# Attention of the prompt's first three heads moved from the gather loop into the input projections, in a one-core transformer step

## The chip, the cores and the metric

The kernel runs on one core of a Trainium2 chip. A core has five engines with instruction queues of their own, each of which takes its instructions in the order written: TensorE (PE; its weight loads are shown as PEld), VectorE (DVE), ScalarE (ACT), GpSimd (POOL) and SyncE (SP, here a queue of DMA issues). The metric is the device time of one execution in microseconds (us); lower is better. The kernel before takes 2638.99 us, the median of three runs (2634.69 to 2639.50).

## The reference

One inference step of a trunk with two layers, for a prompt of 256 tokens and 8 sample sequences of 4 new tokens with a paged cache of 2048 tokens. Layer 0 mixes tokens by sparse attention, layer 1 by a convolution module; each is followed by a convolutional feed-forward network. The change is in layer 0 alone. For the prompt it computes, per block of 128 queries:

```python
p = x @ w_in                              # q (16 heads), k and v (4 heads), qi (16 x 64), ki (64), wi (16)
q, k, qi, ki = rope_all(q, k, qi, ki, pos)
dots  = jnp.einsum('thd,sd->ths', qi, ki)
score = jnp.einsum('th,ths->ts', wi * IDX_W_SCALE, relu(dots))
_, idx = top_k(where(causal, score, -inf), 64)            # each query keeps 64 keys
s = einsum('tngd,tsnd->tngs', q, k[idx]) * HEAD_DIM ** -0.5
o = einsum('tngs,tsnd->tngd', softmax(where(valid, s, -inf)), v[idx])
y = o.reshape(T, 2048) @ w_out
```

For the sample tokens it is the same with 256 selected keys out of 2052 each, which are read from the paged cache by index. Prompt and samples go through all weight matrices together, as 288 columns (256 + 32).

## The kernel before

**Weights.** All weights are fp32 and are multiplied in three passes: a slab of weights (128 x 1024) is loaded (`raw`), split into a high part on ScalarE (`wh`, L166) and a low part on VectorE or, for slabs with the flag `pool`, on GpSimd (`wl`, L168), and multiplied at L245 to L247 (`wh` by the high half of x, `wh` by the low half, `wl` by the high half). `pump` (L142) issues loads up to five slabs ahead and splits up to three ahead.

**Lanes.** The order of instructions is written out by hand (a manual schedule). `gemm` (L258) emits a projection's matmuls and calls `tick` (L184) after every few of them with their planned time. `tick` gives that time as credit to each of a list of lanes. A lane is a queue of generators; each `yield` names the time after which the next piece of work may be emitted between the projection's matmuls. `drain` (L197) emits all that is left in a lane at once.

**Layer 0, projections.** The order is index keys, k (`g_k`), index queries (two groups), q (four groups of 512 columns, one group per key head), v (two groups of 256 columns). A q group has 8 slabs, a v group 4. A group's results are copied out of PSUM by ScalarE (`evac_rope`, L729: staging copies L733, full copies L735), rotated on VectorE (L738 to L743) and copied back by ScalarE (L747). Beside them run as lanes: the prompt's index (`prompt_index`, its top 64 by eight rounds of max and replace, with the mask `pm` at L1083 and L1084), and `sample_index`, which finds for each sample token its 256 best keys: a bisection in 31 steps (L923 on VectorE, a count over partitions on TensorE at L902, L933, L934), then a compaction into a list of row numbers (L941 to L1022), whose last step writes `idxS` (L1029) and calls `kv_load`. After the second v group `drain` finishes these lanes.

**Gathers.** `kv_load` (L771) issues per sample token two gathers of 128 rows of 4 KB (512 KB each) on GpSimd (L672), with a small memset (`pause`, L786) behind each. The buffers are a ring of 11: four of `kvA`, three of `kvB`, and four that lie over xh and xl, the halves of x, once the projections are done. A buffer comes free when the value matmuls of its token are done.

**Layer 0, loop.** For each of 32 sample tokens t (L1351): `keys(t)` transposes the gathered keys on TensorE (L1251, two groups of four) and copies them out (L1254 VectorE, L1256 ScalarE); `scores(t - 1)` multiplies them (L1272); after each four tokens comes a softmax, and `values` (L1315, and L1320 to L1327) emits the products with the gathered values in steps between later tokens. Between these steps `fill(FILL)` emits pieces of `filler` (L1184): the prompt's attention, as eight units of one key head (four query heads) and one tile of 128 tokens. A unit adds the mask and the scores in PSUM (L1200, L1201), takes the row maximum on VectorE (L1202, L1204), the exponential with its row sum on ScalarE (L1206), the reciprocal and the scaling of the weights on VectorE (L1210, L1212), transposes the weights on TensorE (L1227, copied out by ScalarE at L1229), multiplies with the values (L1223) and copies the result out (L1232). In the filler the scores of one unit are emitted ahead of the transposes and the value product of the unit before it. At token 24 `pump` is called for the out-projection; by then two of its slabs have been split during the second v group. After the loop the attention's output is split (L1374, L1375) and the out-projection begins.

Of the kernel before, what the change touches and what calls it, by code (L numbers as in the profile page):

```python
# [39 lines left out]
FILL = 0.45  # L40
# [10 lines left out]
HEAD = 2.0  # L51
# [3 lines left out]
LST = (2.5, 2.5, 2.5, 1.6, 1.2, 0.9)  # L55
# [61 lines left out]
class K:  # L117
    def __init__(self, ctx, tc, a, o):
# [8 lines left out]
        self.slabs = []  # L127
        self.n_dma = self.n_split = self.pos = 0
# [12 lines left out]

    def pump(self, i):  # L142
        nc = self.nc
        while True:
            if self.n_dma < min(len(self.slabs), i + self.R) and self.n_dma < self.n_split + self.R:
                s = self.slabs[self.n_dma]
                r = self.wraw.tile([128, 1024], F32, name="raw")
                v = r[:, :s.kt * s.C].rearrange("p (k c) -> p k c", c=s.C)
                off = 0
                for w, c0, n in s.segs:  # L150
                    src = w[s.k0 * 128:(s.k0 + s.kt) * 128, c0:c0 + n].rearrange("(k p) c -> p k c", p=128)
                    nc.sync.dma_start(v[:, :, off:off + n], src)
                    off += n
                self.raw[self.n_dma] = r
                self.n_dma += 1
            elif self.n_split < min(self.n_dma, i + self.S):
                s = self.slabs[self.n_split]
                n = s.kt * s.C
                r = self.raw.pop(self.n_split)
                if s.plain:  # L160
                    self.sp[self.n_split] = (r, None)
                    self.n_split += 1
                    continue
                wh = self.wsp.tile([128, 1024], F32R, name="wh")
                wl = self.wsp.tile([128, 1024], F32R, name="wl")
                nc.scalar.activation(wh[:, :n], r[:, :n], AF.Copy)  # L166
                eng = nc.gpsimd if s.pool else nc.vector
                eng.tensor_tensor(wl[:, :n], r[:, :n], wh[:, :n].bitcast(F32), op=OP.subtract)  # L168
                if not s.pool:
                    self.v(1.1)  # L170
                self.sp[self.n_split] = (wh, wl)
                self.n_split += 1
            else:
                break
# [376 lines left out]
def trunk(ctx, tc, a, o, stages=9):  # L551
# [72 lines left out]
    stB = ExitStack()  # L624
# [26 lines left out]
    con = bp.tile([128, NCO], F32, name="con")  # L651
# [54 lines left out]
    R = bp.tile([128, 4, T], F32, name="rsh")  # L706
# [61 lines left out]
    kvt = {"pos": 0, "done": 0, "cap": 4}  # L768
    RING = 4 + NKVB + 4

    def kv_load(done):  # L771
        kvt["done"] += done
        while kvt["pos"] < min(kvt["done"] + kvt["cap"], NS * TS):
            t = kvt["pos"]
            i = t % RING
            if i < 4:
                g = kvA.tile([128, 2, 1024], F32, name="kvt")
            elif i in (7, 8, 9):
                g = kvt["B"].tile([128, 2, 1024], F32, name="kvt")
            else:  # L780
                g = kvt["B2"][i // 6][:, i // 5 % 2 if i < 6 else i // 10]
# [67 lines left out]
    def sample_index():  # L849
# [179 lines left out]
        nc.vector.tensor_scalar(idxS, p[:, :64], 0.25, None, op0=OP.add)  # L1029
        kv_load(0)  # L1030
# [4 lines left out]
    def prompt_index(half):  # L1035
# [35 lines left out]
        for tt in range(2):  # L1071
# [14 lines left out]
            yield PRI  # L1086

# [30 lines left out]
    q = base.tile([128, NT, T], F32, name="x")  # L1118

    def post_q(h):  # L1120
        return lambda: nc.scalar.activation(qn[:, h], q[:, 4 * h:4 * h + 4, TP:].rearrange("p g t -> p t g"), AF.Copy)

    for gi in range(4):
# [3 lines left out]
    vT = bp.tile([128, 8, T], F32, name="qi")  # L1127

    def turn_v(gi):

        for tt in range(3):
            n = 128 if tt < 2 else 32
            p = pb()
            for m in range(2):
                nc.tensor.transpose(p[:n, m * 128:m * 128 + 128], vT[:, 2 * gi + m, tt * 128:tt * 128 + n], ident)
            dst = vt[:, tt] if tt < 2 else vs
            nc.scalar.activation(dst[:, 256 * gi:256 * gi + 256], p[:n, :256], AF.Copy)
            yield 0.6

    for gi in range(2):  # L1140
# [8 lines left out]
    nc.sync.dma_start(o["v"][:TP].rearrange("(a p) c -> p a c", p=128), vt)  # L1149
    nc.sync.dma_start(o["v"][TP:], vs)  # L1150
    k.lanes.remove(kxl)
    k.lanes.remove(pl_)
    k.fine = False
    stB.close()
# [4 lines left out]
    stC = ExitStack()  # L1159
    cp = stC.enter_context(tc.tile_pool(name="att", bufs=2))  # L1160
    kvB = stC.enter_context(tc.tile_pool(name="kvB", bufs=NKVB))
# [6 lines left out]
    ot = q  # L1168
# [11 lines left out]
    kvt["B"] = kvB  # L1180
    kvt["B2"], kvt["cap"] = [base.tile([128, 2, 2, 1024], F32, name="kvx", tag=n) for n in ("xh", "xl")], RING
    kv_load(0)

    def filler():  # L1184
        units = [(tt, h) for tt in range(2) for h in range(4)]
        st_ = {}

        def qk(u):
            tt, h = u
            nk = 128 * (tt + 1)  # L1190
            per = 512 // nk
            P = cp.tile([128, 4, nk], F32, name="P")
            mx = cp.tile([128, 4], F32, name="mx")
            sm = cp.tile([128, 4], F32, name="sm")
            for b0 in range(0, 4, per):
# [40 lines left out]
        for n in range(len(units) + 1):  # L1236
            if n < len(units):
                yield from qk(units[n])
            if n:
                yield from pv(units[n - 1])  # L1240
# [688 lines left out]
```

## Time and profile before

| | |
|---|---|
| median of three runs | 2638.99 us |
| the profiled execution | 2612.4 us, of which the span from first to last instruction is 2610.6 us |
| instructions | 49517 |
| mean granted clock of TensorE | 0.993 of full speed |
| TensorE busy, share of the span | 97% |
| VectorE, ScalarE, GpSimd | 62%, 45%, 25% |
| projections of layer 0 | from the start to 272 us |
| loop of layer 0 up to the first out-projection matmul | 272 to 398 us |

The profile is of one execution. Its page gives busy times per engine, a chain of waits followed back from the last instruction, and groups of instructions by line. Rows of the stage view give, for a stretch from A to B, its length, then for PE, PEld, DVE, ACT and POOL the busy time with the number of instructions in brackets, then the granted clock, the busy share of the DMA engines and their rate in GB/s. Rows of a timeline give start, duration, engine, line, operation, and in square brackets how long the engine had been idle and what it had waited for. Rows of groups give line, engine, operation, shapes and count, then total busy time and the mean of one in ns, then idle time ahead of them. Rows of the wait view give who waited for whom: total, number, longest. TensorE's instructions overlap, so that the duration of one is longer than the distance to the next.

### The profile page before, as it was taken

Reading aid. Unit: us, or ns where it says so; the run is one execution under the profiler, and the core shown is the slowest. Engines: PE = TensorE matmul, PEld = TensorE weight load, DVE = VectorE, ACT = ScalarE, POOL = GpSimd, SP = SyncE. Lnnn points to the kernel's source line nnn. Section 1 sums busy time; section 2 is a strip of 40 time slices with the busy share of each in tenths; the row PEclk is TensorE's granted clock in tenths of the full one; section 3 lists DMA queues with packets and bytes.
Section 4 is the critical chain, followed back from the end, with each engine's and each line's share of the span. In section 5 each row is a group of like instructions: output and inputs, shape, how many; then the busy total and the mean of one; then the engine's idle time right before and its main releaser. Section 6 shows DMA issues by size and latency. Waiting matters only on the chain.

```text
span 2610.6 us, 49517 instructions
## 1 busy us (share of the span) xinstructions
PE 2540.9 (97%) x19572; PEld 2445.5 (94%) x19572; DVE 1611.6 (62%) x2525; ACT 1163.7 (45%) x1811; POOL 643.3 (25%) x917
## 2 busy tenths in 40 slices
PE   8999899999999999999998998999999999999997
PEld 8889669999999999999998897999999999999997
DVE  4577446686665445555659887768555444655554
ACT  4444444464443334443446444656444333444334
POOL 2042661442221101011236543343110000111123
PEclk9999999999999999999999999999999999999999
DMA  9935875555555555556555675565555555555653
GB/s 341 205 109 153 298 273 169 164 182 180 166 169 162 154 176 162 168 162 163 172 161 144 166 191 145 178 173 163 170 160 171 160 157 171 163 168 167 162 167 104
DMA packets 410329, 454.91 MB, mean 174 GB/s; under 512 B 34816, under 2 KB 338096, under 8 KB 408944
## 3 DMA queue, kind: packets, MB, share of 16 engines
q1 hardware_dynamic: 397696, 400.66, 51.9%
q0 software_dynamic: 12400, 51.09, 5.8%
q8 instruction: 153, 2.51, 0.4%
q14 instruction: 80, 0.66, 0.1%
HBM read 438.37 MB, written 13.30 MB: 173 GB/s over the span
## 4 chain that ended last, share of the span: by engine, by line
PE 88%; DVE 4%; DMA 3%; POOL 2%; ACT 2%; issue 1%; SPq 1%; ACTq 0%; DVEq 0%; POOLq 0%
PE pt L247 25%; PE pt L246 25%; PE pt L245 25%; PE pg L245 2%; PE pg L247 2%; PE pg L246 2%; DVE wl L168 2%; PE tr L1251 1%; PE pt L1715 1%; ACT wh L166 1%; PE sc L1272 1%; PE m L1315 1%; DMA raw<-w_ffn_down 1%; PE pg L873 1%; POOL x L503 1%
## 5 line engine op out<-in xcount | busy, mean ns | idle before, releaser
L168 DVE TENSOR_TENSOR wl<-raw,wh 128x1024 fp32r<-128x1024 f32 (+1 forms) x707 | 882.0, 1251 | 786.1 <-ACT wh L166 768.3
L166 ACT ACTIVATE wh<-raw 128x1024 fp32r<-128x1024 f32 (+1 forms) x726 | 760.4, 1051 | 903.2 <-PE pt L246 686.3
L247 PE MATMUL pt<-xh,wl 128*128 128x288 f32 (+1 forms) x3520 | 1041.2, 296 | 5.5 <-DVE wl L168 5.4
L245 PE MATMUL pt<-xh,wh 128*128 128x288 f32 (+1 forms) x3520 | 1043.0, 296 | 0.8 <-ACT xh L1374 0.8
L246 PE MATMUL pt<-xl,wh 128*128 128x288 f32 (+1 forms) x3520 | 1043.0, 296 | 0.1
L247 PEld LDWEIGHTS pt<-xh,wl 128*128 128x128 f32 x3520 | 666.9, 189 | 7.3 <-DVE wl L168 7.3
L245 PEld LDWEIGHTS pt<-xh,wh 128*128 128x128 f32 x3520 | 664.2, 189 | 7.4 <-issue 5.8
L246 PEld LDWEIGHTS pt<-xl,wh 128*128 128x128 f32 x3520 | 664.5, 189 | 0.5 <-DVE xl L1375 0.3
L247 PE MATMUL pt<-hh,wl 128*128 128x288 f32 (+1 forms) x1664 | 495.5, 298 | 3.2 <-DVE wl L168 3.2
L245 PE MATMUL pt<-hh,wh 128*128 128x288 f32 (+1 forms) x1664 | 493.2, 296 | 1.2 <-ACT wh L166 1.2
L246 PE MATMUL pt<-hl,wh 128*128 128x288 f32 (+1 forms) x1664 | 494.2, 297 | 0.0
L1490 POOL COPY sto<-gpad 128x2 f32<-128x2 f32 x88 | 82.0, 932 | 962.1 <-ACT gpad L1483 962.0
L247 PEld LDWEIGHTS pt<-hh,wl 128*128 128x128 f32 x1664 | 312.8, 188 | 4.4 <-DVE wl L168 4.4
L245 PEld LDWEIGHTS pt<-hh,wh 128*128 128x128 f32 x1664 | 313.6, 188 | 2.3 <-ACT wh L166 2.1
L246 PEld LDWEIGHTS pt<-hl,wh 128*128 128x128 f32 x1664 | 313.7, 189 | 0.2
L245 PE MATMUL pg<-xh,wh 128*128 128x288 f32 (+1 forms) x528 | 166.3, 315 | 7.9 <-ACT wh L166 7.9
L247 PE MATMUL pg<-xh,wl 128*128 128x288 f32 (+1 forms) x528 | 157.4, 298 | 1.7 <-DVE wl L168 1.6
L246 PE MATMUL pg<-xl,wh 128*128 128x288 f32 (+1 forms) x528 | 157.5, 298 | 0.0
L1494 ACT ACTIVATE s<-y,pvec 128x304 f32<-128x304 f32 x88 | 48.4, 550 | 161.4 <-DVE y L1489 161.4
L245 PEld LDWEIGHTS pg<-xh,wh 128*128 128x128 f32 (+1 forms) x528 | 100.0, 189 | 17.9 <-issue 9.3
L247 PEld LDWEIGHTS pg<-xh,wl 128*128 128x128 f32 (+1 forms) x528 | 99.9, 189 | 3.0 <-DVE wl L168 3.0
L246 PEld LDWEIGHTS pg<-xl,wh 128*128 128x128 f32 (+1 forms) x528 | 99.8, 189 | 3.0 <-issue 2.4
(353 smaller groups left out, 2281.0 us busy)
## 6 DMA issues: line engine op xcount, KB each, us to landing
raw<-w_ffn_gate SPq DMA_DIRECT2D x352, 256.0 KB, 2.9
raw<-w_ffn_up SPq DMA_DIRECT2D x352, 256.0 KB, 3.2
raw<-w_ffn_down SPq DMA_DIRECT2D x169, 512.0 KB, 3.8
raw<-w_attn_in SPq DMA_DIRECT2D x64, 512.0 KB, 5.8
raw<-w_pw SPq DMA_DIRECT2D x128, 256.0 KB, 4.7
raw<-w_attn_out SPq DMA_DIRECT2D x32, 512.0 KB, 4.1
raw<-w_pw SPq DMA_DIRECT2D x32, 512.0 KB, 4.3
xt<-spread SPq DMA_DIRECT2D x60, 136.0 KB, 2.9
```

The costliest lines, as they stand in the source:

```text
L166: nc.scalar.activation(wh[:, :n], r[:, :n], AF.Copy)
L168: eng.tensor_tensor(wl[:, :n], r[:, :n], wh[:, :n].bitcast(F32), op=OP.subtract)
L245: nc.tensor.matmul(out, wh[:, c:c + w], xh, start=st, stop=False)
L246: nc.tensor.matmul(out, wh[:, c:c + w], xl, start=False, stop=False)
L247: nc.tensor.matmul(out, wl[:, c:c + w], xh, start=False, stop=sp)
L503: nc.gpsimd.tensor_tensor(x[:, i - 1], x[:, i - 1], rs, op=OP.mult)
L873: nc.tensor.matmul(p[:, :512], qb[:, pr], kx[pr][:, 512 * i:512 * i + 512], start=True, stop=True)
L1251: nc.tensor.transpose(p[:, h * 128:(h + 1) * 128], g[:, h * 128:(h + 1) * 128], ident)
L1272: nc.tensor.matmul(p[32 * h:32 * h + 16, :KSEL_S], qz[b % 2][:, i, h], kt[:, h], start=False, stop=(i == TS - 1), skip_group_check=True)
L1315: nc.tensor.matmul(po[32 * h:32 * h + 16, :128], z[:, c, i, h], g[:, 512 + h * 128:640 + h * 128], start=False, stop=(i == TS - 1 and c == ...
L1490: nc.gpsimd.tensor_copy(sto[:, j, 0:2], gp[:, 256:258])
L1494: nc.scalar.activation(s[:, :304], y[:, :304], AF.Silu, bias=k.par(bc, j))
```

## The change

The order of the groups becomes index keys, k, index queries, q0, v (both groups), q1, q2, q3. GpSimd still splits 18 slabs, the first 18 behind q0. The v groups are evacuated into the rotation buffer `R`, transposed in a lane of their own (`tv`), and stored from there.

The attention of a unit becomes a function of its own, `unit`, with a list of yields (`gap`), in which the weights are scaled on ScalarE instead of VectorE. A lane `at` runs `prompt_heads`: as soon as the mask, the values and the sample index's dot products are there, it takes two buffers of `kvA` and runs both units of head h once the q group h is rotated, for h = 0, 1, 2, with a yield of 2.4 after each score bank, 1.6 ahead of the transposes and after each of them, and 0.8 at the end. `filler` in the loop keeps head 3 alone, without the overlap of neighbouring units, and is called with a smaller `FILL` and no head start.

The selection's buffers (`sel`, `idx`) are closed at the end of `sample_index`, and `kvB` is opened there, so that the gathers of five tokens can be issued at that point (`cap` 5 in place of 4); the rest of the ring follows after the projections. The constants `con` and `R` move into a pool of their own that lives until the end of the projections. The yields of the list (`LST`) become shorter. A bar keeps `pump` from splitting out-projection slabs during q3; a fifth slab is loaded after the drain, and at tokens 23, 26 and 29 of the loop one slab each is split and another loaded.

```diff
-FILL = 0.45
+FILL = 0.13
+GAP = (2.4, 1.6, 1.6, 0.8)
...
-HEAD = 2.0
+HEAD = 0.0
...
-LST = (2.5, 2.5, 2.5, 1.6, 1.2, 0.9)
+LST = (2.2, 2.2, 2.2, 1.45, 1.2, 0.8)
...
-            elif self.n_split < min(self.n_dma, i + self.S):
+            elif self.n_split < min(self.n_dma, i + self.S, self.bar):
...
-    g_q = [k.add(Group([(win, QC + 512 * i, 512)], [128] * 4, NT, 2)) for i in range(4)]
+    g_q = [k.add(Group([(win, QC, 512)], [128] * 4, NT, 2))]
     g_v = [k.add(Group([(win, VC + 256 * i, 256)], [128] * 2, NT, 4)) for i in range(2)]
-    for g in g_q[1:]:
-        for s_ in g.slabs[:8 if g is not g_q[3] else 2]:
-            s_.pool = True
+    g_q += [k.add(Group([(win, QC + 512 * i, 512)], [128] * 4, NT, 2)) for i in range(1, 4)]
+    for s_ in g_v[0].slabs + g_v[1].slabs + g_q[1].slabs + g_q[2].slabs[:2]:
+        s_.pool = True
...
         nc.vector.tensor_scalar(idxS, p[:, :64], 0.25, None, op0=OP.add)
+        k.drain(pl_)
+        stB.close()
+        kvt["B"] = stC.enter_context(tc.tile_pool(name="kvB", bufs=NKVB))
+        kvt["cap"] = 2 + NKVB
         kv_load(0)
...
+    def project_q(gi):
         ps = k.gemm(g_q[gi], xin, pg)
+        k.drain(tv)
         evac_rope(2 * gi + 2, ps, [q[:, 4 * gi + m] for m in range(4)], post_q(gi))
...
+    def unit(tt, h, P, PT, mx, sm, bank_, bank_o, gap):
...
+            for i in range(per):
+                nc.scalar.activation(P[:, b0 + i], p[:, i * nk:(i + 1) * nk], AF.Exp,
+                                     bias=mx[:, b0 + i:b0 + i + 1], scale=SCALE,
+                                     accum_out=sm[:, b0 + i:b0 + i + 1])
+            yield gap[0]
+        nc.vector.reciprocal(sm, sm)
+        for i in range(4):
+            nc.scalar.activation(P[:, i], P[:, i], AF.Identity, scale=sm[:, i:i + 1])
+        yield gap[1]
...
+    def prompt_heads():
+
+        while not (masked and vdone and dots_done):
+            yield 0.5
+        Pb, Pt = (kvA.tile([128, 2, 1024], F32, name="kvt") for _ in range(2))
+        for h in range(NKV - 1):
+            while h not in roped:
+                yield 0.3
+            for tt in range(2):
+                P = Pb[:, tt, :512 * (tt + 1)].rearrange("p (a b) -> p a b", a=4)
+                yield from unit(tt, h, P, [Pt[:, 0, 512 * i:512 * i + 512] for i in range(2)],
+                                Pt[:, 1, 8 * tt:8 * tt + 4], Pt[:, 1, 8 * tt + 4:8 * tt + 8], pb, pb, GAP)
+
+    project_q(0)
     for gi in range(2):
         ps = k.gemm(g_v[gi], xin, pg)
         for m in range(2):
-            nc.scalar.activation(vT[:, 2 * gi + m], ps[m][:, :T], AF.Copy)
-        if gi:
-            k.drain(k.ev, k.bg2, kxl, pl_, k.bg)
-        pl_.append(turn_v(gi))
-    k.drain(pl_)
...
+            nc.scalar.activation(R[:, 2 * gi + m], ps[m][:, :T], AF.Copy)
+        tv.append(turn_v(gi))
+    at.append(prompt_heads())
+    project_q(1)
+    project_q(2)
+    k.bar = g_out[0].first
+    project_q(3)
+    kvt["B2"] = [base.tile([128, 2, 2, 1024], F32, name="kvx", tag=n) for n in ("xh", "xl")]
+    k.drain(k.ev, k.bg2, kxl, pl_, k.bg, at)
+    k.load()
+    k.bar = 1 << 30
...
-    kvt["B2"], kvt["cap"] = [base.tile([128, 2, 2, 1024], F32, name="kvx", tag=n) for n in ("xh", "xl")], RING
+    kvt["cap"] = RING
     kv_load(0)
...
-        if t == n_t - 8:
-            k.pump(g_out[0].first)
+        if t in (n_t - 9, n_t - 6, n_t - 3):
+            k.split()
+            k.load()
```

More of the change, by code (lines that the diff above doesn't have):

```diff
@@ L140, in add, with load, split @@
         return g
+    def load(self):
+        s = self.slabs[self.n_dma]
+        r = self.wraw.tile([128, 1024], F32, name="raw")
+        v = r[:, :s.kt * s.C].rearrange("p (k c) -> p k c", c=s.C)
+        off = 0
+        for w, c0, n in s.segs:
+            src = w[s.k0 * 128:(s.k0 + s.kt) * 128, c0:c0 + n].rearrange("(k p) c -> p k c", p=128)
+            self.nc.sync.dma_start(v[:, :, off:off + n], src)
+            off += n
+        self.raw[self.n_dma] = r
+        self.n_dma += 1
+    def split(self):
+        nc = self.nc
+        s = self.slabs[self.n_split]
+        n = s.kt * s.C
+        r = self.raw.pop(self.n_split)
+        if s.plain:
+            self.sp[self.n_split] = (r, None)
+            self.n_split += 1
+            return
+        wh = self.wsp.tile([128, 1024], F32R, name="wh")
+        wl = self.wsp.tile([128, 1024], F32R, name="wl")
+        nc.scalar.activation(wh[:, :n], r[:, :n], AF.Copy)
+        eng = nc.gpsimd if s.pool else nc.vector
+        eng.tensor_tensor(wl[:, :n], r[:, :n], wh[:, :n].bitcast(F32), op=OP.subtract)
+        if not s.pool:
+            self.v(1.1)
+        self.sp[self.n_split] = (wh, wl)
+        self.n_split += 1
@@ L704, in trunk @@
     SHUF_I = [i ^ 8 if i < 16 else i for i in range(32)]
-    R = bp.tile([128, 4, T], F32, name="rsh")
+    R = bl.tile([128, 4, T], F32, name="rsh")
     turned = []
@@ L766, in trunk @@
     k.ev.append(rope(kiw[0:64], R[0:64, 0], cc("ci", 0, 64), cc("si", 0, 64), SHUF_I, post_ki))
-    kvt = {"pos": 0, "done": 0, "cap": 4}
+    kvt = {"pos": 0, "done": 0, "cap": 0}
     RING = 4 + NKVB + 4
@@ L1115, in trunk, with post @@
     k.bg.append(sample_index())
-    q = base.tile([128, NT, T], F32, name="x")
+    q = ot = base.tile([128, NT, T], F32, name="x")
+    tv, at = Lane(), Lane()
+    k.lanes += [tv, at]
     def post_q(h):
-        return lambda: nc.scalar.activation(qn[:, h], q[:, 4 * h:4 * h + 4, TP:].rearrange("p g t -> p t g"), AF.Copy)
-    for gi in range(4):
+        def post():
+            nc.scalar.activation(qn[:, h], q[:, 4 * h:4 * h + 4, TP:].rearrange("p g t -> p t g"), AF.Copy)
+            roped.append(h)
+        return post
+    def project_q(gi):
         ps = k.gemm(g_q[gi], xin, pg)
+        k.drain(tv)
         evac_rope(2 * gi + 2, ps, [q[:, 4 * gi + m] for m in range(4)], post_q(gi))
-    vT = bp.tile([128, 8, T], F32, name="qi")
     def turn_v(gi):
@@ L1177, in trunk @@
         nc.vector.memset(t, 0.0)
-    kvt["B"] = kvB
-    kvt["B2"], kvt["cap"] = [base.tile([128, 2, 2, 1024], F32, name="kvx", tag=n) for n in ("xh", "xl")], RING
+    kvt["cap"] = RING
     kv_load(0)
     def filler():
[L1185 to L1192, printed above, removed]
+        h = NKV - 1
+        for tt in range(2):
+            P = cp.tile([128, 4, 128 * (tt + 1)], F32, name="P")
+            PT = [cp.tile([128, 512], F32, name="PT", bufs=2) for _ in range(tt + 1)]
@@ L1236, in filler @@
[L1236 to L1240, printed above, removed]
+            yield from unit(tt, h, P, PT, mx, sm, lambda: bank("tr", 3),
+                            lambda: bank("q", 1), (1.1, 0.6, 0.6, 0.9))
     KT, SC = {}, {}
```

132 lines of the change are left out of this document (53 added, 79 removed).

## The prediction

> **What bounds the kernel now.** I read the page first, then the busy time of each engine by stage, then the chain of waits at the hand-over from projections to attention loop, then the timelines of GpSimd and TensorE there.
>
> ```profile
> PE 2540.9 (97%) x19572; PEld 2445.5 (94%) x19572; DVE 1611.6 (62%) x2525; ACT 1163.7 (45%) x1811; POOL 643.3 (25%) x917
> PE 88%; DVE 4%; DMA 3%; POOL 2%; ACT 2%; issue 1%; SPq 1%; ACTq 0%; DVEq 0%; POOLq 0%
> ```
>
> TensorE is busy 97% of the span and carries 88% of the chain. Work moved from one place to another on TensorE is therefore worth nothing in itself; only TensorE's waits are. The stages, with PE, PEld, DVE, ACT and POOL busy, then granted clock and DMA share:
>
> ```profile
> 188.00:217.00 29.00, 28.60 (x217) 27.42 (x216) 19.97 (x92) 14.16 (x24) 19.54 (x9) 1.00 0.52 147
> 217.00:246.00 29.00, 25.73 (x194) 25.21 (x193) 24.24 (x47) 12.37 (x20) 0.00 (x0) 1.00 0.53 145
> 246.00:272.20 26.20, 26.20 (x199) 25.92 (x198) 20.51 (x38) 13.93 (x24) 0.00 (x0) 1.00 0.39 121
> 272.20:288.20 16.00, 8.55 (x54) 6.32 (x53) 6.67 (x21) 6.40 (x24) 13.39 (x21) 0.79 0.84 303
> 288.20:398.20 110.00, 104.49 (x1318) 65.25 (x1318) 52.83 (x145) 45.03 (x123) 69.40 (x108) 1.00 0.78 288
> ```
>
> The first three rows are the projections (third q group, fourth, both v groups), the fifth is the loop to the first out-projection matmul. TensorE waits 16 - 8.55 = 7.45 us at the hand-over, 110 - 104.49 = 5.5 us in the loop, 3.3 us in the fourth q group. The chain says what the hand-over waits for:
>
> ```profile
> 272.24 0.38 PE pg L1027 x4
> 272.64 0.24 DVE idxS L1029
> 273.15 1.06 POOL kvt L672
> 277.62 10.41 DMA kvt<-kvc,idxS
> 288.16 0.63 PE tr L1251 x4
> ```
>
> The list of sampled keys is finished only by the drain at the end of the v groups; then come the gathers and their landing. The loop's other pacemaker is the gather queue:
>
> ```profile
> 274.72 0.97 POOL L672 DMA_INDIRECT kvt<-kvc,idxS  x1 [0.17 <-issue]
> 377.41 0.94 POOL L672 DMA_INDIRECT kvt<-kvc,idxS  x1 [0.17 <-issue]
> POOL kvt L672 <- PE m L1315: 10.1, 5, 3.6
> POOL kvx L672 <- PE m L1315: 3.4, 2, 2.4
> ```
>
> From the second gather to the 64th are 102.7 us; 13.5 of them are waits for a ring buffer that TensorE's value matmuls free, so 62 gathers cost (102.7 - 13.5) / 62 = 1.44 us each.
>
> **The change part by part.** *The moved attention.* A unit is a head and a 128-token tile. Its TensorE work, in the loop:
>
> ```profile
> 288.62 0.22 PE L1200 MATMUL tr<-pm,identN 128*128 128x128 bf16 x1
> 288.96 0.22 PE L1200 MATMUL tr<-pm,identN 128*128 128x128 bf16 x1
> 361.72 0.28 PE L1200 MATMUL tr<-pm,identN 128*128 128x256 bf16 x1
> 362.27 0.27 PE L1200 MATMUL tr<-pm,identN 128*128 128x256 bf16 x1
> 293.20 0.65 PE tr L1227 x4
> 295.44 0.86 PE q L1223 x2
> ```
>
> Four score pairs are 0.34 apart in the first tile and 0.55 in the second, four transposes take some 0.6, a value product 0.86. First tile: 1.35 + 0.6 + 0.86 = 2.8 us; second: 2.2 + 1.2 + 1.7 = 5.1 us. Three heads are 24 us, which leave the loop and enter the projections: sum zero. The projections would end at 272.2 + 24 = 296 plus new waits.
>
> *The hand-over wait.* The list's pacing constants shrink, and 24 us of other work lie ahead of the projections' end, so it is done before it. By order: v groups give the lanes 6 ticks a slab where q groups give 8, so the list loses some 6 us in them, and is held up by two heads' matmuls (16 us in part); it regains 3 us from the shorter yields. I put its end at 273 to 285 against an end of the projections near 302. The first pair of gathers needs 1.44 us and the chain's 10.4 us of landing, and the others follow faster than the loop takes them; so up to 290 it is early enough. The 7.45 us go, and with them the low clock after them:
>
> ```profile
> 280.00:284.00 4.00, 0.00 (x0) 0.00 (x0) 1.65 (x8) 2.48 (x10) 3.51 (x7) 0.53 1.01 379
> 284.00:288.00 4.00, 3.29 (x10) 1.90 (x10) 0.69 (x1) 0.92 (x2) 3.51 (x7) 0.62 1.04 417
> ```
>
> At a clock of 0.62, 3.29 us busy are worth 2.0: 1.3 us. Together -8.75 us (bounds -8.75 and 0, the latter if the list were late).
>
> The Trainium skill, "TensorE: Matmul & The Clock Gate", Part 1, says that the clock halves after an idle window of about 3.4 us; the two rows agree (0.53 and 0.62 behind a wait of over 4 us). By that rule the new wait below, about as long, might bring half of that loss back.
>
> *The new wait at the hand-over.* The fourth q group now comes last, and the loop's first filler unit and first scores need its rotated queries. Behind it stand the evacuation and the rotation:
>
> ```profile
> 246.23 1.32 ACT L735 ACTIVATE x<-pg 128x288 f32<-128x288 f32 x4
> 249.67 0.48 DVE L738 STREAM_SHUFFLE rsh<-rsh 128x288 f32<-128x288 f32 x1
> 251.05 0.46 DVE L743 TENSOR_TENSOR rsh<-rsh 128x288 f32<-128x288 f32 x1
> 251.60 1.84 ACT L747 ACTIVATE x<-rsh 32x288 f32<-32x288 f32 x4 [1.67 <-DVE rsh L743]
> ```
>
> The rotation takes 251.51 - 249.67 = 1.84 us on VectorE, the copy back 1.84 on ScalarE, the last bank's staging some 0.5: 4.2 us after the last matmul. One set of key transposes (0.6) and what is left of the third head cover part. +3 us (bounds 0, if a whole unit is left over, and 4.2).
>
> *New waits inside the projections.* This decides the sign. In the loop the next unit's scores lie between a unit's scores and its transposes; in the lane there is only the pace: 2.4 + 1.6 = 4.0 of planned time, which is 4.36 us because three matmuls are planned at 0.3675 and the third row above has eight slabs of 24 matmuls in 26.2 us, 0.4 for three. TensorE takes instructions in order: if the scaled weights are late, all projection matmuls behind the transposes wait. The chain:
>
> ```profile
> L1202 DVE TENSOR_REDUCE mx<-tr 128x2 f32<-128x512 f32 x8 | 5.5, 689 | 8.4 <-PE tr L1201 8.3
> L1206 ACT ACTIVATE P<-tr,mx 128x128 f32<-128x128 f32 x8 | 2.8, 366 | 5.3 <-PE tr L1251 3.5 <-DVE mx L1204 1.8
> L1206 ACT ACTIVATE P<-tr,mx 128x256 f32<-128x256 f32 x16 | 7.4, 470 | 19.3 <-DVE mx L1204 8.4 <-DVE qz L1357 3.6 <-DVE KT L1254 3.0
> L1210 DVE RECIPROCAL sm<-sm 128x4 f32<-128x4 f32 x6 | 1.0, 167 | 0.4 <-ACT P L1206 0.4
> L1212 DVE TENSOR_SCALAR P<-P,sm 128x256 f32<-128x256 f32 x16 | 5.8, 425 | 0.1
> L487 ACT ACTIVATE x<-x,pvec x48: 612/615/638, 522.7 to 1787.4; 128x288 f32<-128x288 f32 x48
> L1229 ACT ACTIVATE PT<-tr 128x512 f32<-128x512 f32 x11 | 6.6, 601 | 7.6 <-PE tr L1227 7.6
> L166 ACT ACTIVATE wh<-raw 128x1024 fp32r<-128x1024 f32 (+1 forms) x726 | 760.4, 1051 | 903.2 <-PE pt L246 686.3
> L168 DVE TENSOR_TENSOR wl<-raw,wh 128x1024 fp32r<-128x1024 f32 (+1 forms) x707 | 882.0, 1251 | 786.1 <-ACT wh L166 768.3
> ```
>
> First tile: reduce 0.7, and 0.3 by estimate for its small multiply and the hand-over, four exponentials 1.5 to 1.7, reciprocal 0.3, four scalings. The trace has no scaling on ScalarE; between 0.37 (the exponential) and 0.6 (Identity with scale on 288 columns) I take 0.4 at 128 and 0.5 at 256 columns: 1.6 and 2.0 us. That is 4.5 us for the first tile, 4.4 for the second (two exponentials behind the last scores): just the pace. But a slab split of 1.05 us stands on ScalarE ahead of the scalings in most units (a slab every 3.2 us, a gap of 2.6), and on VectorE a split of 1.25 or a step of the list may be ahead of the reduce. About 1 us each unit, so 6 units give +5.5 us. Bounds: -3.3, if the pauses give VectorE the air that the fourth q group lacks in its row (25.73 of 29) and nothing else waits; +14, if both splits hit each unit (2.3 each). I take the middle since VectorE is 69 to 84% busy in these rows. ScalarE has room: eight exponentials, eight scalings and five copies out of PSUM at 0.6 are some 11 us a head, on top of 12 to 14 us in 29.
>
> *The loop.* Of the last two rows' work, 8.55 - 1.3 + 104.49 = 111.75 us, TensorE keeps 87.75. Its 5.5 us of waits become 4, since fewer softmaxes stand in its way: -1.5 (bounds -3 and 0). With the wait for the queries it needs 3 + 87.75 + 4 = 94.75 us from the projections' end. GpSimd has 54 gathers x 1.44 = 77.6 us from there, and behind the last one stand between 10.4 us (landing alone) and 20.8 (377.4 to 398.2 now, where TensorE was behind as well): 88 to 98.4. The two are level, and each hands waits to the other through the ring: +1 us (bounds 0, and 6 if GpSimd takes the upper end and some ring waits stay).
>
> *Edits at no cost.* The same 18 slabs after q0 go to GpSimd in the same places. The out-projection's first splits move from the v groups into the loop (two more pairs of 1.05 and 1.25 us), where ScalarE and VectorE are under half busy, with four 512 KB loads more at a DMA share of 0.78. The stores of v move up SyncE's queue, ahead of loads for which five buffers stand in store. One row shows a side effect:
>
> ```profile
> 366.18 1.93 POOL L672 DMA_INDIRECT kvx<-kvc,idxS  x1 [0.16 <-issue]
> 366.07 1.22 DVE L168 TENSOR_TENSOR wl<-raw,wh 128x1024 fp32r<-128x1024 f32 x1 [1.56 <-ACT wh L166]
> ```
>
> A gather under a split takes 1 us longer. Two more such collisions in the loop are within the +1. "GPSIMD Engine Reference", section 8, of the Trainium skill says that GpSimd shares its SBUF interfaces with VectorE, with contention under two-input instructions; the pair of rows agrees, and the rule speaks against moving splits into the stretch where GpSimd issues the gathers.
>
> Sum: -8.75 + 3 + 5.5 - 1.5 + 1 = -0.75 us on the profiled execution of 2612.4 (its span 2610.6), which lies 26.6 below the median of the runs. I carry the difference over: 2639.0 - 0.75 = 2638.2.
>
> **The rivals.** *A: the pace suffices* (0.30). The units' waits come to 0 and the loop stays TensorE's: -8.75 + 3 + 0 - 1.5 + 0 = -7.25, 2631.7; with the lower bounds of the other terms -8.75 + 0 - 3.3 - 3 = -15, 2624. For it: the chain without neighbours just fits 4.36 us; ScalarE is at 50%. Against: splits every 3.2 us.
> *B: the moved softmaxes stall the projections* (0.17). Slower: one wait per unit, PE's transposes for ScalarE's scaled weights. It decides from about 2 us a unit: 12.5 instead of 5.5 gives +6.25, 2645; with 14, and 3 us of ring waits, 2649. For it: VectorE at 84% there already, and TensorE did wait 3.3 us in the fourth q group. Against: pauses give VectorE and ScalarE time.
> *C: the list is late* (0.05), the change's aim missed: the early gathers don't land before the loop, 4 to 8 us of the wait stay: 2642 to 2646. It decides from a list that ends after 290. Against: 5 to 17 us of margin.
>
> **How the numbers follow.** A measurement here can tell about 0.2%, 5.3 us. My forecast, no change, has 0.48, its own range 2634 to 2644. Faster 0.30 (A), slower 0.22 (B and C). The range reaches to 2627 (A, more than half of the way to its lower bound) and 2649 (B's upper end).
>
> **What would show it.** Right: gathers start before the last projection matmul; no DMA wait at the first keys; the projections end at 300 to 304; a wait of some 3 us for the rotated queries; some 1 us of TensorE wait on ScalarE per unit; the loop 93 to 97 us from there; few ring waits of the gathers; the out-projection starts at 395 to 400. Wrong: projections ending by 297 (A) or after 308 (B), first gather after 295 (C), or a clock below 1 in the projections.

## The result and the profile after

The changed kernel takes 2660.97 us (median of 4 runs, 2660.18 to 2663.43) where the kernel before takes 2638.01 on the same chip (2634.69 to 2639.50): 1.009 times as long, 95% interval 1.0073 to 1.0108. Slower by some 23 us; my forecast was no change.

The chips on which the runs fell differ by 1%: before takes 2612 to 2613 us on some and 2635 to 2638 on others, so every ratio here is against before on the same chip. On a chip of the quicker kind, like that of the profile in the prediction, after takes 2639.25 against 2611.80 (1.0105, 1.0088 to 1.0122); its profile, "after_third" below, is read first, since its rows can be held against the prediction's one by one.

From its page, the busy share of each engine and the chain that ended last by engine:

```profile
PE 2554.7 (97%) x19572; PEld 2452.9 (93%) x19572; DVE 1600.7 (61%) x2493; ACT 1175.2 (45%) x1843; POOL 642.4 (24%) x917
PE 86%; DVE 4%; POOL 4%; ACT 2%; DMA 2%; issue 1%; SPq 1%; ACTq 0%; POOLq 0%; DVEq 0%
```

The same number of matmuls, and TensorE as busy as before (97%); its share of the chain falls from 88% to 86%, GpSimd's rises from 2% to 4%. Busy time by stage in after_third (length, PE, PEld, DVE, ACT, POOL, granted clock, DMA share, GB/s): three rows of projections, then the loop:

```profile
188.00:222.00 34.00, 33.45 (x240) 30.37 (x238) 22.39 (x100) 16.17 (x37) 18.95 (x9) 1.00 0.51 158
222.00:274.00 52.00, 43.06 (x258) 36.94 (x259) 29.75 (x74) 25.60 (x58) 0.78 (x1) 0.90 0.28 81
274.00:321.50 47.50, 40.23 (x242) 35.12 (x241) 22.92 (x49) 20.45 (x49) 3.96 (x6) 0.89 0.29 91
321.50:426.00 104.50, 90.78 (x1235) 55.93 (x1235) 44.60 (x117) 40.53 (x100) 78.62 (x122) 0.98 0.89 332
```

The projections end at 321.5 in place of 272.2: 49.2 us later, of which 24 are the moved work. The rest is idle time and clock. TensorE is idle for 0.55 + 8.94 + 7.27 = 16.8 us in the first three rows, against 3.7 in the prediction's three (84.2 - 80.53), 13.1 more. The clock of 0.90 and 0.89 costs 5.2 + 5.2 = 10.4 us at most (the rows count idle time too), where all three rows of before had 1.00. The loop is 126.0 - 104.5 = 21.5 us shorter. The remainder after it is 2211.9 us against 2212.3. Together 49.2 - 21.5 - 0.4 = 27.3 us, the difference of the two spans (2637.9 and 2610.6).

What the projections wait for, and where the list comes, are seen at one unit in after_third. These are timeline rows (start, duration, engine, line, operation, and in brackets the idle time ahead), with TensorE's projection matmuls left out:

```profile
305.60 1.06 ACT L167 ACTIVATE wh<-raw 128x1024 fp32r<-128x1024 f32 x1
306.69 1.23 DVE L169 TENSOR_TENSOR wl<-raw,wh 128x1024 fp32r<-128x1024 f32 x1 [1.26 <-ACT wh L167]
307.83 0.42 DVE L1031 COPY_PREDICATED slot<-ob,slot 128x256 f32<-128x256 int32 x1
308.17 0.17 DVE L1187 RECIPROCAL kvt<-kvt 128x4 f32<-128x4 f32 x1
308.43 1.71 ACT L1189 ACTIVATE kvt<-kvt 128x256 f32<-128x256 f32 x4 [1.77 <-DVE kvt L1187]
...
309.00 1.53 PE L1201 MATMUL pg<-ident,kvt 128*128 128x128 f32 x4 [1.99 <-ACT kvt L1189]
...
316.01 0.53 PE L1036 MATMUL pg<-con,slot 128*128 128x32 f32 x4
316.58 0.22 DVE L1038 TENSOR_SCALAR idxS<-pg 128x64 int32<-128x64 f32 x1 [8.24 <-PE pg L1036]
```

A slab's split stands on ScalarE and then on VectorE; the unit's 0.17 us reciprocal has to wait behind both and behind a step of the list, ScalarE's scalings wait for the reciprocal, and TensorE's transposes for the scalings. They then run at the pace of the scalings, 0.4 us apart. All projection matmuls behind them wait too. The same fence shows the list: its last VectorE step ends at 308.25, but its four matmuls (L1036) stand in TensorE's queue behind this unit and run at 316, so `idxS` waits 8.24 us.

The wait view of after_third from 180 to 322 us (who waits for whom: total, number, longest):

```profile
ACT kvt L1183 <- DVE kvt L1180: 17.3, 6, 3.7
PEld pg L1201 <- ACT kvt L1189: 15.7, 15, 4.1
PE pg L1201 <- ACT kvt L1189: 12.2, 4, 3.9
```

By this view the transposes' waits are 12.2 of the 13.1 us of new idle time. They come from four of the six units: 3.89, 2.65, 3.62 and 1.99 us, at the units of heads 1 and 2. The two units of head 0 cost TensorE no such wait; the slabs beside them were split on GpSimd (its last split starts at 220.40), those beside the other four on VectorE, which fits the chain above. The clock falls behind each of the four: it is 0.50 or 0.51 from 242.5 to 245, 263 to 266, 290.5 to 296 and 311 to 314 us. The last of these rows, TensorE busy throughout:

```profile
311.00:314.00 3.00, 3.00 (x12) 2.48 (x12) 0.00 (x0) 0.16 (x1) 0.00 (x0) 0.51 0.03 7
```

A clock of 0.51 after a unit's waits, with work at hand. The Trainium skill, "TensorE: Matmul & The Clock Gate", Part 1, says that the gate judges free-running windows of about 3.4 us and halves the clock after an idle one. The half agrees; the idle window does not, since the wait ahead of this row was 1.99 us and the one at 262 was 2.65. How much of a window must be idle, no run here shows.

The loop, on GpSimd's timeline: first and last gather, and the chain through that stretch by line:

```profile
317.09 1.06 POOL L681 DMA_INDIRECT kvt<-kvc,idxS  x1 [94.31 <-DVE idxS L1038]
...
408.84 0.94 POOL L681 DMA_INDIRECT kvt<-kvc,idxS  x1 [0.17 <-issue]
```

```profile
by line: DMA kvt<-kvc,idxS 23.2%; POOL kvt L681 20.6%; POOL kvx L681 16.2%; POOL pause L795 12.6%; PE tr L1289 8.3%; issue 7.1%; PE m L1353 4.2%; PE sc L1310 2.6%; PE q L1196 1.1%; PE tr L1176 0.9%; PE m L1346 0.8%; PE pg L1036 0.4%; PE tr 
```

64 gathers back to back take 91.75 us from the first to the last, with no ring wait over 0.2 us among them. Behind the last one stand 425.97 - 408.84 = 17.1 us. The chain is no longer TensorE's: GpSimd with its pauses and the gathers' landing carry 73% of it. The same view of before, on a chip of the same kind (before_again, 276 to 379 us):

```profile
by line: PE tr L1251 24.9%; PE sc L1272 11.6%; PE m L1315 10.3%; DMA kvt<-kvc,idxS 10.0%; PE tr L1201 8.1%; PE q L1223 7.9%; PE tr L1227 4.8%; ACT P L1206 3.4%; PE tr L1200 2.4%; PE m L1308 2.0%; POOL kvt L672 1.9%; PE sc L1264 1.5%; issue 
```

There TensorE's lines lead. (Each view covers the stretch from about the first gather to the last.)

### The profile page after: what moved, and what is told of

The parts are those of the page before. It is cut to its first block, busy times and chain, and to the rows that moved or that the text cites. A ratio compares the mean times of both kernels' runs of the same rounds, so it can differ in the third digit from the quotient of the medians.

```text
span 2659.4 us, 49529 instructions
## 1 busy us (share of the span) xinstructions
PE 2564.3 (96%) x19572; PEld 2456.6 (92%) x19572; DVE 1602.8 (60%) x2493; ACT 1175.1 (44%) x1843; POOL 640.0 (24%) x917
## 4 chain that ended last, share of the span: by engine, by line
PE 87%; DVE 4%; POOL 2%; ACT 2%; DMA 2%; issue 1%; SPq 0%; another core or an unknown queue 0%; ACTq 0%; DVEq 0%; POOLq 0%
PE pt L254 25%; PE pt L253 25%; PE pt L255 25%; PE pg L253 2%; PE pg L255 2%; PE pg L254 2%; DVE wl L169 2%; PE pt L1754 1%; ACT wh L167 1%; PE tr L1289 1%; PE m L1353 1%; DMA raw<-w_ffn_down 1%; PE pg L882 1%; PE sc L1310 1%; POOL x L511 0%
## 5 line engine op out<-in xcount | busy, mean ns | idle before, releaser
L253 PE MATMUL pg<-xh,wh 128*128 128x288 f32 (+1 forms) x528 | 172.9, 328 | 8.1 <-ACT wh L167 8.1
L253 PEld LDWEIGHTS pg<-xh,wh 128*128 128x128 f32 (+1 forms) x528 | 102.1, 193 | 21.5 <-issue 12.4
L1533 ACT ACTIVATE s<-y,pvec 128x304 f32<-128x304 f32 x88 | 48.4, 550 | 162.0 <-DVE y L1528 162.0
```

The lines of the kernel that those rows point to most:

```text
L253: nc.tensor.matmul(out, wh[:, c:c + w], xh, start=st, stop=False)
L1533: nc.scalar.activation(s[:, :304], y[:, :304], AF.Silu, bias=k.par(bc, j))
```

## The experiments

Lines of the edits are those of the kernel named. Ratios are to before on the same chip, with 95% intervals.

**The kernel before again**, for its profile: no edit.

> The kernel before, unchanged, for a second profile: the first one is of an execution 26 us below the median of the timed runs. If the stages of layer 0 are what differs, this profile should show projections that end after 272 us or a loop longer than 126 us; if not, the difference lies behind layer 0, and both profiles can be compared with the changed kernel's stage by stage up to the out-projection.

1.0003 (0.9993 to 1.0012), 2612 us. Its projections end at 273.6, the first gather is at 274.55, the last at 379.26, the out-projection starts at 400.11. So the profile of the prediction is repeatable on that kind of chip.

**What the loop can earn.** Before, with heads 0 to 2 of the prompt's attention left out of the computation and nothing put elsewhere:

```diff
-FILL = 0.45
+FILL = 0.13
-HEAD = 2.0
+HEAD = 0.0
-        units = [(tt, h) for tt in range(2) for h in range(4)]
+        units = [(tt, h) for tt in range(2) for h in range(NKV - 1, NKV)]
```

> The kernel before with the prompt's attention of heads 0 to 2 left out altogether (their part of the output is not computed), filler paced for the one head left. If the loop is set by TensorE (theory of the prediction), 24 us of work less make it 20 to 24 us shorter, ratio 0.991. If it is set by the ring of gather buffers (new theory: gather, landing, keys, values, buffer free again), the loop stays within 6 us of its 126 us and the gathers wait longer for buffers: ratio 0.998 to 1.000.

0.9937 (0.9921 to 0.9954), 16.1 us less; a second time 0.9932 (0.9915 to 0.9948), 18.9 less:

> The kernel before with the prompt attention of heads 0 to 2 left out, as in loop_one_head, beside the others. It bounds what the moved work can earn. Theory L: 16 to 23 us less than before, not 24 plus the waits that lie between the units. Rival T: 24 us or more.

24 us of TensorE work left out are worth 16 to 19: less than the 20 to 24 that the first theory gave, more than the 6 of the second. The first run's GpSimd rows say why:

```profile
274.70 1.07 POOL L672 DMA_INDIRECT kvt<-kvc,idxS  x1 [57.16 <-DVE idxS L1029]
...
366.51 0.95 POOL L672 DMA_INDIRECT kvt<-kvc,idxS  x1 [0.17 <-issue]
```

91.8 us, as in after: the same back-to-back issue. It is a floor under the loop's end (first gather + 92 + 17), and before lay some 17 us above it. Work moved out of the loop cannot earn more, wherever it goes, unless the first gather also comes sooner.

**The gathers' issue, halved.** In after and in before, the second gather of each token becomes a plain load of 128 rows on SyncE's queue: the same bytes, other rows, so the sample attention reads other keys and values.

```diff
             for c in range(2):
-                gather(g[:, c], a["kvc"], idxS[:, 32 * c + t:32 * c + t + 1])
+                if c:
+                    nc.sync.dma_start(g[:, c], a["kvc"][128 * t:128 * t + 128])
+                else:
+                    gather(g[:, c], a["kvc"], idxS[:, 32 * c + t:32 * c + t + 1])
```

> half_gathers again: after with half of the gathers as plain loads on SyncE's queue (other rows). On the quicker chip, theory G (GpSimd's issue of 92 us is the floor of after's loop): 4 to 12 us less than after, the loop down towards its TensorE work of 88 us and waits. Rival (its transfers are): within 3 us of after. On the other chip: 26 us less than after, as before.

> before_half again: before with half of the gathers as plain loads on SyncE's queue (other rows). On the quicker chip: 0.999 times before, as it was. On a chip where before takes 2635 us, theory H2 (what makes that chip's loop 21 us longer is the gathers' queue): 15 to 25 us less than before, the loop at 125 to 130 us. Rival: within 5 us of before, and the chip's loss lies elsewhere.

On the quicker chip after gets 5.4 us faster (2633.88 against after_third's 2639.25; 1.0086, 1.0069 to 1.0103, so the intervals overlap), its loop by the profiles 98.2 us in place of 104.5, and the ring waits of before come back:

```profile
POOL kvt L681 <- PE m L1356: 17.6, 6, 6.0
POOL kvx L681 <- PE m L1356: 5.2, 3, 2.7
```

Before does not move: 0.9993 (0.9984 to 1.0003), and the same on an earlier chip, 0.9993 (0.9983 to 1.0002):

> The kernel before, with the second of each token's two gathers replaced by a plain load of 128 rows of the same cache on SyncE's queue, as in half_gathers (the sample attention reads other rows). Theory H (the gathers on GpSimd's queue hold before's loop too, so TensorE work taken out of it is partly taken out of waits): the loop shortens by 15 us or more, 0.990 to 0.995 times before. Rival T (before's loop is held by TensorE, 112 us of work, and the gathers hide behind it): within 5 us of before.

So on these chips before's loop is not held by GpSimd's issue, and after's is, by some 6 us over what holds it next: the change took the loop from one bound to the next. On a chip of the slower kind after itself lost far more by the edit, 2634.88 against 2662.54, as fast as before (0.9999, 0.9989 to 1.0008):

> after, with the second of each token's two gathers replaced by a plain load of 128 rows of the same cache on SyncE's queue: the same bytes, half of GpSimd's gathers (so the sample attention reads other rows). Theory G (GpSimd's 1.44 us a gather is the floor of the loop): GpSimd's 92 us of issue become 46, the loop shortens by 8 to 12 us to TensorE's own work and waits, time 8 to 12 us under after. Theory B (the 33.6 MB themselves are the floor): the loop stays within 4 us of after's.

27.7 us where theory G gave 8 to 12; the loop is 101.0 us there, nearly the 98.2 of the quicker chip. So the gathers on GpSimd's queue hold up more there than their issue time.

**The units' chain.** In after, the reciprocal and the scalings are emitted directly behind the last exponentials, ahead of the yield:

```diff
-            yield gap[0]
+            if b0 + per < 4:
+                yield gap[0]
         nc.vector.reciprocal(sm, sm)
         for i in range(4):
             nc.scalar.activation(P[:, i], P[:, i], AF.Identity, scale=sm[:, i:i + 1])
-        yield gap[1]
+        yield gap[0] + gap[1]
```

> The changed kernel with each unit's reciprocal and scaling emitted right behind its last exponentials, ahead of the yield, so that no slab split stands between them on ScalarE and VectorE. Theory: exponentials, then split on ScalarE, then split on VectorE, then reciprocal, then scalings is the chain that makes TensorE wait 2 to 4 us in each unit; without the two splits in it the projections' end comes 8 to 15 us earlier (2646 to 2653). Rival: the softmax is too slow for the pace in itself; less than 4 us change.

1.0085 (1.0068 to 1.0102), against after's 1.0105 on another quick chip; the intervals overlap. In its profile the transposes' waits fall from 12.2 us to 2.3, and the projections end at 310.4, 11 us sooner, as the theory had it. Its stage from 188 us on, and rows of its wait view there:

```profile
188.00:310.40 122.40, 110.26 (x733) 97.85 (x731) 74.51 (x215) 61.55 (x142) 23.06 (x14) 0.97 0.37 114
PE pg L911 <- DVE scr L932: 7.9, 5, 2.6
PE pg L1202 <- ACT kvt L1190: 2.3, 4, 1.0
```

Not all of the waits are gone: TensorE now waits 7.9 us for VectorE at the bisection's counts (L911), where after_third had 2.7. All idle time in the projections falls only from 16.8 us to 12.1 (122.40 - 110.26). The clock of 0.97 costs 3.7 us at most in place of 10.4, so the larger part of the 11 us is the clock. Then `unit` cut in two, `soft` (to the scalings) and `weigh` (transposes and value product), so that the next unit's scores lie between them, as in the loop of before:

```diff
+        late = None
         for h in range(NKV - 1):
+            if late and h not in roped:
+                yield from weigh(*late)
+                late = None
...
-                yield from unit(tt, h, P, [Pt[:, 0, 512 * i:512 * i + 512] for i in range(2)],
-                                Pt[:, 1, 8 * tt:8 * tt + 4], Pt[:, 1, 8 * tt + 4:8 * tt + 8], pb, pb, GAP)
+                u = (tt, h, P, [Pt[:, 0, 512 * i:512 * i + 512] for i in range(2)],
+                     Pt[:, 1, 8 * tt:8 * tt + 4], Pt[:, 1, 8 * tt + 4:8 * tt + 8], pb, pb, GAP)
+                yield from soft(*u)
+                if late:
+                    yield from weigh(*late)
+                late = u
+        yield from weigh(*late)
```

> The lane's units overlap: the scores of the next unit are issued ahead of the transposes and P V of the one before, nothing else is changed. Theory S (the projections are stalled because a unit's transposes stand in TensorE's queue right behind its own softmax): projections end 299-304 in place of 310, first gather 6 to 10 us sooner, and the whole 6 to 10 us faster than after (2622 to 2627). Rival (the stalls are the splits' waits for ScalarE and VectorE, which carry the softmaxes in either order): projections end 307 or later and the time is within 3 us of after.

> The changed kernel, nothing edited, for a profile on the same chip as the kernel before and the variants. Theory S+L (serial units stall the projections by some 13 us over the 24 us of moved work; the loop cannot end sooner than first gather + 64 gathers at 1.44 us + some 17 us, so it gives back at most 17 us): projections end 308-312, first gather 304-307, the loop from there about 110 us, 1.008 to 1.010 times before. Rival R (the loop is held by ring slots, as in the first profile of after with its 14.5 us of ring waits): the ring waits are here too, the loop is 120 us or more and the out-projection starts after 425.

Both fell on a chip of the slower kind: 2649.42 us against 2662.54 for after beside it (1.0055, 1.0038 to 1.0072, against 1.0104, 1.0087 to 1.0121): 13.1 us faster, the intervals apart, and 9.7 between the two profiled executions. after_again itself was as rival R had it and not as S+L: projections end at 318.8, first gather at 314.4, ring waits of 15.6 and 6.3 us, a loop of 126.7 us. Stages of lane_pipelined:

```profile
188.00:222.00 34.00, 34.00 (x254) 31.65 (x252) 23.05 (x104) 17.70 (x41) 19.72 (x9) 1.00 0.51 158
222.00:272.00 50.00, 44.11 (x303) 39.22 (x303) 34.47 (x80) 29.19 (x66) 0.00 (x0) 1.00 0.36 106
272.00:308.00 36.00, 29.69 (x186) 26.63 (x185) 16.97 (x37) 14.69 (x37) 3.24 (x5) 0.91 0.27 88
```

The projections end at 308.0 in place of 318.8, and the clock is back at 1.00 up to 272. So a stall of serial units is shown, at 11 us with its clock; theory S had hoped for an end at 299 to 304. In these rows 12.2 us of idle time stay (3.7 in before's). Half of it is one wait in the new order:

```profile
291.35 1.70 ACT L1189 ACTIVATE kvt<-kvt 128x256 f32<-128x256 f32 x4 [2.24 <-DVE kvt L1187]
292.95 0.57 ACT L1207 ACTIVATE kvt<-pg 128x512 f32<-128x512 f32 x1
293.58 2.08 PE L1199 MATMUL pg<-kvt,vt 128*128 128x512 f32 x2 [6.31 <-ACT kvt L1207]
```

The value product of a unit waits 6.31 us for the copy of its transposed weights, which now stands on ScalarE behind the next unit's softmax and scalings. The overlap took the wait away from the transposes and put one at the value product.

**The list sooner**, in lane_pipelined:

```diff
-LST = (2.2, 2.2, 2.2, 1.45, 1.2, 0.8)
+LST = (1.1, 1.1, 1.1, 0.7, 0.6, 0.4)
```

> lane_pipelined with the list's pace halved (each pause of the list's steps half as long), so that it is ready sooner against the projections' end. Theory C (the list comes late, and gathers with it, which bound the loop): idxS and the first gather 10 to 14 us sooner than in lane_pipelined, ten gathers issued before the projections end, and the whole 4 to 10 us faster than lane_pipelined (1.002 to 1.004 times before). Rival (the list's own VectorE work then stalls the splits, or the ring of five tokens ends the gain): the first gather comes sooner, the time is within 2 us of lane_pipelined (1.005 to 1.006) or above.

1.0038 (1.0024 to 1.0052) against 1.0055 (1.0038 to 1.0072), on another chip of the slower kind: intervals overlap. Seven gathers are issued before the projections end, not ten. The first gather comes 6.9 us sooner (297.51 against 304.43), the last only 0.9 sooner (414.01 against 414.95), and the out-projection too (433.65 against 434.57). Five tokens of ring are filled in 14 us and the rest waits for the loop. By the profile the list's lateness alone is worth about 1 us, by the medians up to 5; its share stays open.

**The rest of the change.** after with all four heads back in the loop, as serial units:

```diff
-FILL = 0.13
+FILL = 0.52
...
-    at.append(prompt_heads())
...
-        h = NKV - 1
-        for tt in range(2):
+        for tt, h in [(tt, h) for tt in range(2) for h in range(NKV)]:
```

> The changed kernel with no head in the projections and all four in the loop (one unit after the other, as in the changed filler); order of the groups, early end of the selection's buffers, split places and scaling on ScalarE as changed. Theory: the projections lose the 24 us of moved work and the 22 us of waits, and the loop, set by the ring, stays near 126 us: 2610 to 2640, as before. Rival: the new order itself (q3 last, list later, splits in the loop) costs the time: 2645 or more.

1.0081 (1.0064 to 1.0098). It is 19.0 us slower than before on a quick chip. The projections end at 275.7, 2 us later than before's 273.6 in before_again, so of the 25 us that after's projections take beyond the moved work all but some 3 come with the units in the lane. But the loop takes 138.9 us against 126.5, where the theory had 126. From its wait view, 272 to 415 us:

```profile
POOL kvt L681 <- PE m L1351: 13.1, 5, 4.3
PEld tr L1201 <- ACT P L1189: 11.2, 25, 1.7
POOL kvx L681 <- PE m L1351: 8.2, 3, 4.2
```

The transposes wait for the scalings here as in the lane, and the ring for TensorE. With the overlapped `filler` of before (VectorE scalings, `FILL` 0.45, `HEAD` 2.0) in its place:

> All four heads in the loop with the overlapped units and VectorE scaling of the kernel before; kept of the change: the order of groups, the early pools and gathers, the out-projection's splits. Theory U (what heads_back lost, 12 us in the loop, was the units' overlap): the loop is back at 122-127 us and the time at 2608 to 2614, level with before. Rival O (the order of the groups, the late rope of q3 and the splits in the loop cost it): still 2620 or more.

1.0018 (1.0009 to 1.0028), 4.9 us over before, on a slower chip, so the forecast of 122 to 127 us for the loop is not tested (154.6, in the slowest of its ten runs, against 147.8 in before_pair below). So the order of groups, early pools and splits in the loop cost about 5 us together. Serial units in the loop cost some 14 to 17 more (19.0 against 4.9, or 1.0081 against 1.0018); overlap, scaling on VectorE and the pacing changed in one edit there, so the share of each is not shown.

**The pauses between gathers.** after without the memset:

```diff
                 gather(g[:, c], a["kvc"], idxS[:, 32 * c + t:32 * c + t + 1])
-
-                nc.gpsimd.memset(pause, 0)
```

> after without the 0.34 us memset that stands behind each gather on GpSimd. Theory G (GpSimd's issue is the floor of the loop): a gather takes 1.1 us, 64 of them 70 us, the loop shortens by 5 us or more and the time is 5 us or more under after (1.007 or less). Theory B (the gathers' transfers are the floor, or what their traffic holds up): no gain, within 3 us of after, or slower.

Slower, not faster: 2674.42, 1.0147 (1.0128 to 1.0166), where after took 2662.38 on that chip. Rows of its timeline:

```profile
341.24 0.60 ACT L1293 ACTIVATE KT<-tr 128x512 f32<-128x512 f32 x1 [10.68 <-remote]
...
347.53 1.29 DVE L1291 COPY KT<-tr 128x512 f32<-128x512 f32 x2 [12.61 <-remote]
```

ScalarE and VectorE stand still for over 10 us each, released by nothing that the trace shows (`remote`). Theory G's gain did not come. Thinned out in before, with a second memset behind each gather:

```diff
                 nc.gpsimd.memset(pause, 0)
+                nc.gpsimd.memset(pause, 0)
```

> The kernel before, with a second 0.34 us memset behind each gather: 64 x 1.78 us is 114 us, still under the loop's length. Theory D (bursts of gathers stop ScalarE and VectorE for microseconds; without the pauses after became 12 us slower): fewer such stops, the loop 3 to 12 us shorter on a chip where it takes 148 us, none or little where it takes 127. Rival (the ring decides, and each gather later is a loss): slower by 2 to 10 us.

1.0044 (1.0030 to 1.0058), 10.5 us slower, the rival's way (2 to 10) and not theory D's, though not by the ring: 64 gathers take 122.5 us (the forecast had 114) with no ring wait over 0.4 us among them, and they bound the loop. One pause more and one less both lose, but in two kernels and on two kinds of chip: for one kernel on one chip it is not shown.

**The pair on a slower chip.** No edit, one run each:

> The kernel before, for a profile on the same chip as the one of after taken next to it. Theory L: its projections end at 271 to 275, its loop is longer than after's by 17 to 22 us and no more, though 24 us of TensorE work more lie in it, and the rest from the out-projection on is the same within 1 us. Rival R2: the loops differ by 24 us or more, and the whole loss lies in the projections.

> The changed kernel beside it. Theory L: projections end 36 to 46 us later than in before_pair (24 us of moved work and 12 to 22 us of stalls), the loop 17 to 22 us shorter, the out-projection starts 15 to 25 us later. Rival R2: as much as 24 us shorter or more.

Projections end at 272.3 and 320.7, the loops take 147.8 and 124.6 us, the spans are 2632.8 and 2660.5. GpSimd's waits in before_pair, then in after_pair:

```profile
POOL kvt L672 <- PE m L1315: 25.7, 6, 10.6
POOL kvx L672 <- PE m L1315: 10.2, 6, 4.8
```

```profile
POOL kvt L681 <- PE m L1353: 13.0, 5, 4.7
POOL kvx L681 <- PE m L1353: 5.8, 4, 2.7
```

The loss has the same make here (+48.4 in the projections, -23.2 in the loop, +2.5 behind it; theory L had 36 to 46 and 17 to 22), though the floor of 109 us from the first gather isn't reached (129.0) and ring waits stay. Before's loop is 21 us longer than on the quicker chips and the stage before it is not; nearly all of that chip's difference lies there. Why, is open, but the traces narrow it. In the loops of eight of the nine profiles from slower chips ScalarE or VectorE stands still at least once, for 3.6 us or more, with `remote` as the only releaser (3.88 us in before_pair, 6.59 in after_pair). In none of the eleven from quicker chips does either do so for over 0.3 us. The ninth slower one is half_gathers, the one with half of the gathers off GpSimd's queue. These stops are too short to make up the 21 us by themselves, and before_half, which would test it in before, fell twice on quicker chips.

## Why the prediction was wrong

- *New waits inside the projections* is the step that failed. I put +5.5 us, about 1 us a unit, bounded by +14 "if both splits hit each unit (2.3 each)". The runs show 49.2 - 24 = 25.2 us: 13.1 of idle time, up to 10.4 of slow clock, the rest unassigned. The idle time alone is within my bound of 14; with the clock it is not. Four waits at the transposes make 12.2 us, 3 us each and 3.9 at most, more than the 2.3 that I allowed: one split passes through both engines, and the reciprocal and the scalings wait behind it in turn. Taking those waits away (scale_first, lane_pipelined) wins back 11 of the 25.2 us; the other 14, most of which also come with the units in the lane (heads_back), have no experiment of their own. I had priced the wait and not the clock behind it, though I quoted the row at 0.62. I also named the overlap of neighbouring units as what the lane lacks, and still took the middle.
- *The hand-over wait*: I put the list's end at 273 to 285. `idxS` is written at 316.8. Each stall of the projections also delays the list, whose pace is counted in planned TensorE time, and its last matmuls waited 8.2 us in TensorE's queue behind a unit, a wait I had not listed. Three gathers are issued ahead of the projections' end, not ten.
- *The loop*: forecast 95.75 us from the projections' end (94.75 and the +1), measured 104.5. My own GpSimd sum, 54 gathers and 10.4 to 20.8 us of tail, had the right price of a gather; with 61 left it is 61 x 1.44 = 87.8 and a tail of 17.1, which is the 104.5 within 0.5. I called the two bounds level and added 1 us; the floor was the loop.
- The sum by these sizes: -0.75 + 19.7 (waits) + 8.7 (loop) - 0.4 (remainder) = +27.3, the difference measured on the quicker chip.
- *Right*: the moved work's 24 us are sum zero on TensorE; few ring waits on the quicker chip (none over 0.2 us in after_third); no wait for the first keys' gather, and 1.83 + 0.35 us for the rotated queries where I put 3. But on the slower chip of the first result the ring waits are there (14.5 and 6.8 us in after). *Rival B* had the mechanism and its engine, transposes waiting for ScalarE's scaled weights, at half the price: 25.2 / 6 = 4.2 us a unit with the clock, against 2.3 at most. *Rival C's* condition held as well (first gather after 295), but list_sooner shows little to gain by it alone. The signs that I gave for "wrong" all appeared: an end after 308, a first gather after 295, a clock below 1.

No version that computes the same beats before; heads_back_pipe and list_sooner come nearest, at 1.0018 and 1.0038.

## What to carry to other kernels

Before moving work out of a stage, work out the next floor under that stage: here 64 gathers x 1.44 us and a tail of 17, so 24 us of work left out earned 16 to 19. A softmax dropped serially into a dense stream of matmuls can cost its whole chain through the other engines' queues, and then the clock; keep the next unit's scores ahead of the last one's transposes, and look that the copies behind those transposes don't then stand behind the next softmax. Anything that a later stage waits for should not stand in TensorE's queue behind such a unit.

## What the runs showed of the hardware

- A gather of 128 rows of 4 KB costs GpSimd 0.94 to 0.95 us in the median, plus 0.17 of issue and 0.33 for the memset, in after_third with landings of 4.2 to 8.4 us and in before with 5.4 to 11.1.
- Gathers issued without a pause (no_pause) were accompanied by stops of ScalarE and VectorE of 10.7 and 12.6 us without a visible releaser, and a loss of 12 us. Shorter ones, up to 6.6 us, stand in the loops of slower chips with the pause too, and none on quicker chips. That such stops come from the gathers' traffic is argued, not shown.
- Two kinds of chip gave 126 and 148 us for the same loop of the same kernel, with the same projections.
